# Two weight-sum additions per matrix made on GpSimd, in a two-layer decoder trunk with a seven-product feed-forward

## The chip, the cores and the metric

One core of a Trainium2 chip runs the whole program in one launch. The metric is device time in microseconds of that core, from the start of the program to its end. Five engines work side by side and meet through semaphores: TensorE (PE in the profile, with its weight loads as PEld), VectorE (DVE), ScalarE (ACT), GpSimd (POOL) and SyncE (SP). SyncE only issues transfers here; GpSimd issues transfers too, above all those that add what they bring to what lies in the tile already.

## The reference: what is computed

Two layers of a decoder trunk on 512 tokens of 1024 features, in float32. Each layer has a mixer stage (pooling, convolution and block-sparse attention behind one input projection) and then a feed-forward stage. Only the feed-forward is touched:

```python
h2 = rmsnorm(x, norm2_w) * (1 + sc2) + sh2
x = x + g2 * ((jax.nn.silu(h2 @ w_gate) * (h2 @ w_up)) @ w_down)
```

`w_gate` and `w_up` are 1024 x 2816, `w_down` is 2816 x 1024.

## The kernel before

Activations lie transposed, features on the 128 partitions and the 512 tokens along a row. Float32 products are made of three matmuls: every operand is split into a high part that TensorE takes exactly (`whi`, `hi`) and the rest (`wlo`, `lo`), and `mm3` (L157 issues the matmul) multiplies high by high, high by low and low by high. A weight tile holds eight blocks of 128 x 128. `split_w` makes the parts: ScalarE copies the tile to `whi` (L407), VectorE subtracts that from the tile to get `wlo` (L410). There are five `whi` and five `wlo` buffers, so ScalarE can split a tile only when TensorE has left the one five tiles back. Activations are split by `split_from` in the same way (L678 on ScalarE, L679 on VectorE).

**The feed-forward's parts.** The 22 column blocks of gate and up are worked off in four parts (`PARTS`). Most columns are taken two at a time by `glu_pair`: both matrices' 2 x 2 block products are made by seven half-size products in place of eight. Such a *pair* needs sums of weight blocks. The parts have one, three, two and three pairs, in each of the two layers: 18 pairs in all. Ten of them have another pair behind them, eight are the last of their part; behind those come the down products of the part.

**A pair on TensorE.** `glu_pair` runs 14 groups, for gate and up in turn: B21, B11, R1, -V, B22, T3, T4. A group is twelve matmuls on 256 columns. The products accumulate in PSUM banks `e`, `a` and `c`. Between them the banks are read and combined: L1430 and L1439 copy `a` on ScalarE, L1436 copies `c`, L1431, L1445 and L1449 add a bank to a tile on VectorE. L1449 reads the bank `a` after T3 and T4 then goes on accumulating in that same bank, first gate's, then up's. Then follow SiLU (L1457, L1458, L1459 on ScalarE) and the products with up (L1460, L1462, L1463 on VectorE), and the split of the result (L678, L679).

**The weight sums.** `Sums` makes four of the weight tiles of one matrix of a pair. `begin` lets GpSimd fetch one block row into half of `s12` and half of `s43` (L268) and add another to each on the way (L270). `first` fetches the raw blocks of the first tile on SyncE's queue and makes the two other halves with two additions on VectorE, 128 x 512 each: L276 adds raw blocks to the transferred sum, L277 adds the other raw blocks to that result. `first` is called once for gate and once for up, so a pair has four such additions and the program 72. `s12` is then split as the third and fourth weight tile of the pair (one for each matrix), `s43` as the fifth and sixth; the first two and the seventh are raw.

**What orders the work.** Each engine runs its instructions in the order in which a scheduler put them. Instructions wrapped in `pin` keep the order of the program among themselves, on their engine; the others are placed where the scheduler expects them to be ready. The additions were pinned on VectorE, as are the subtractions L410. A weight tile is loaded four tiles ahead of its use, and `begin` of a pair runs up to five tiles ahead of its first tile. The tiles `s12` and `s43` share six buffers (`w4`), the raw tiles three (`RAW`), so a transfer waits until the splits have left the buffer.

Of the kernel before, what the change touches and what calls it, by code (L numbers as in the profile page):

```python
# [85 lines left out]
def hybrid_trunk(ctx, tc, xT, ws, ada, cols, pool_w, qk_w, crow, pos, con, out):  # L86
    nc = tc.nc
    V, A, T = nc.vector, nc.scalar, nc.tensor
# [70 lines left out]
    def pin(ins):  # L159
        return tc.keep_in_program_order(ins)  # L160
# [83 lines left out]
    def fetch(tile, l, blocks):  # L244
        for i, n, src in runs(l, blocks):
            nc.sync.dma_start(tile[:, i:i + n].rearrange("p b n -> p (b n)"), src)
# [5 lines left out]
    class Sums:  # L252
# [19 lines left out]
        def first(self):  # L272
            raw = rawt()
            fetch(raw, self.l, self.blocks(0, 0) + self.blocks(1, 0))
            flat = raw.rearrange("p (g b) n -> p g (b n)", g=2)
            pin(V.tensor_add(self.s12[:, 1], self.s12[:, 0], flat[:, 0]))  # L276
            pin(V.tensor_add(self.s43[:, 0], self.s12[:, 1], flat[:, 1]))  # L277
            return split_w(raw, C_BLOCKS)

        def sums(self, which):  # L280
# [121 lines left out]
    def rawt():  # L402
        return wp.tile([P, C_BLOCKS, P], F32, tag="raw", name=nm("raw"), bufs=RAW)

    def split_w(raw, n):
        hi = wp.tile([P, C_BLOCKS, P], F32R, tag="whi", name=nm("whi"), bufs=5)
        A.activation(hi[:, :n], raw[:, :n], AF.Copy)  # L407
        lo = wp.tile([P, C_BLOCKS, P], F32R, tag="wlo", name=nm("wlo"), bufs=5)
        with tc.issue_after(hold[0].ins) if hold[0] is not None else nullcontext():
            ins = V.tensor_sub(lo[:, :n], raw[:, :n], f32(hi)[:, :n])  # L410
        pin(ins)
        return hi, lo
# [541 lines left out]
    for l in range(L):  # L954
# [438 lines left out]
        def make_forms(c):  # L1393

            h1, h2 = norm.h[c], norm.h[HK + c]
            one, two = bigt(F32), bigt(F32)
            t3, r1 = one[:, :BLOCK], one[:, BLOCK:]
            nv, t4 = two[:, :BLOCK], two[:, BLOCK:]
            V.tensor_sub(t3, h2[:, BLOCK:], h1[:, BLOCK:])
            V.tensor_sub(r1, h1[:, :BLOCK], h1[:, BLOCK:])  # L1400
            V.scalar_tensor_tensor(nv, t3, -1.0, h1[:, :BLOCK], op0=ALU.mult, op1=ALU.subtract)
            V.scalar_tensor_tensor(t4, nv, -1.0, h2[:, :BLOCK], op0=ALU.mult, op1=ALU.subtract)
            (a, al), (b, bl) = split_from(one), split_from(two)
            first, later = slice(0, BLOCK), slice(BLOCK, S)
            k1, k2 = norm.k(c), norm.k(HK + c)
            forms.append({"B11": cut(k1, slice(None), first), "B21": cut(k2, slice(None), first),
                          "B22": cut(k2, slice(None), later),
                          "T3": (a[:, first], al[:, first]), "R1": (a[:, later], al[:, later]),
                          "-V": (b[:, first], bl[:, first]), "T4": (b[:, later], bl[:, later])})
# [216 lines left out]
```

## Time and profile before

| | |
|---|---|
| median of two runs | 1433.36 us (1433.31 to 1433.4) |
| profiled execution, first to last instruction | 1431.7 us |
| median less that span | 1.7 us |
| granted TensorE clock in that execution | 1.000 |
| moved by the DMA engines | 245.51 MB, 171 GB/s on average |

A row of instructions in the profile reads: line, engine, operation, what it writes `<-` what it reads (the program's names), partitions x elements, how many; then busy time and the mean ns of one, and the idle time of the engine ahead of them with what ended it. A row of the timeline starts with the start time and the length in us; `x2` after it means two such instructions in a row, of which the length runs from the first start to the last end. Matmuls overlap each other, so a matmul's own length (0.28 us) is longer than the step from one start to the next, 0.12 us. A row of a window has the busy us of PE, PEld, DVE, ACT and POOL with the number of instructions, then the granted clock, the share of the DMA engines and GB/s.

### The profile page before, as it was taken

What the parts mean: (1) busy time and instruction counts of PE and PEld (TensorE: products, weight loads), DVE (VectorE), ACT (ScalarE), POOL (GpSimd) and SP (SyncE); (2) the same over time, 40 slices, a digit from 0 to 9 for tenths busy, and PEclk for the clock granted to TensorE, in tenths of its full rate; (3) what the DMA queues carried; (4) which work ended last, traced back from release to release, by engine and by line L of the source; (5) the groups of instructions that cost most, each with busy time, mean ns of one, the idle gap of its engine ahead of it and who ended that gap; (6) DMA issues with size and microseconds to landing.
All of it is one profiled execution on the core that took longest, in us unless ns stands there. A gap on an engine that the chain in (4) does not pass through costs nothing.

```text
span 1431.7 us, 22037 instructions
## 1 busy us (share of the span) xinstructions
PE 1426.4 (100%) x8340; PEld 1258.8 (88%) x8340; DVE 1038.3 (73%) x1904; ACT 731.3 (51%) x1229; POOL 153.2 (11%) x215
## 2 busy tenths in 40 slices
PE   9999999999999999999999999999999999999999
PEld 8888888888988998989988888888889989999997
DVE  8887777649686767677788996655878747657663
ACT  5635666733653452535454675666336525435450
POOL 0000110101100311211002000010020103111200
PEclk9999999999999999999999999999999999999999
DMA  9547876765346766756537665567672537636522
GB/s 372 207 147 210 217 189 164 191 220 164 91 141 217 192 175 206 186 144 207 187 103 234 174 152 143 133 163 179 257 206 85 141 103 193 175 105 176 139 89 83
DMA packets 92378, 245.51 MB, mean 171 GB/s; under 512 B 11752, under 2 KB 24432, under 8 KB 92272
## 3 DMA queue, kind: packets, MB, share of 16 engines
q1 hardware_dynamic: 67312, 177.37, 36.4%
q0 software_dynamic: 24368, 66.60, 23.3%
q8 instruction: 65, 1.06, 0.3%
q14 instruction: 41, 0.34, 0.1%
q10 hardware_dynamic: 592, 0.14, 0.0%
HBM read 241.97 MB, written 2.10 MB: 170 GB/s over the span
## 4 chain that ended last, share of the span: by engine, by line
PE 99%; DMA 0%; DVE 0%; SPq 0%; ACT 0%; issue 0%; DVEq 0%; ACTq 0%
PE mm L157 84%; PE pair L157 13%; PE mm L163 2%; DMA x<-in_xT 0%; SPq L203 0%; DVE w L513 0%; ACT big L665 0%; DVE big L917 0%; DVE big L907 0%; DVE tmp L661 0%; DVE x L1313 0%; ACT rst L932 0%; DVE rst L935 0%; DVE rst L934 0%; DVE rst L936 0%
## 5 line engine op out<-in xcount | busy, mean ns | idle before, releaser
L157 PE MATMUL mm<-big,whi 128*128 128x512 f32 (+1 forms) x4334 | 1072.9, 339 | 0.0
L157 PEld LDWEIGHTS mm<-big,whi 128*128 128x128 f32 x4334 | 741.4, 190 | 85.2 <-issue 2.6
L157 PE MATMUL mm<-big,wlo 128*128 128x512 f32 (+1 forms) x2167 | 732.0, 338 | 0.0
L157 PEld LDWEIGHTS mm<-big,wlo 128*128 128x128 f32 x2167 | 411.1, 190 | 45.0 <-issue 0.4
L407 ACT ACTIVATE whi<-raw 128x1024 fp32r<-128x1024 f32 (+2 forms) x190 | 195.9, 1034 | 199.3 <-PE mm L157 112.2
L410 DVE TENSOR_TENSOR wlo<-raw,whi 128x1024 fp32r<-128x1024 f32 (+2 forms) x190 | 223.5, 1187 | 43.8 <-ACT whi L407 43.3
L407 ACT ACTIVATE whi<-w 128x1024 fp32r<-128x1024 f32 x78 | 82.5, 1058 | 150.9 <-PE mm L157 91.5
L1313 DVE SCALAR_TENSOR_TENSOR x<-mm,mod,x 128x512 f32<-128x512 f32 (+1 forms) x89 | 61.5, 693 | 76.4 <-PE mm L157 76.3
L410 DVE TENSOR_TENSOR wlo<-w,whi 128x1024 fp32r<-128x1024 f32 x78 | 94.0, 1221 | 30.4 <-ACT whi L407 29.7
L513 DVE SCALAR_TENSOR_TENSOR w<-w,csil 128x1024 f32<-128x1024 f32 x80 | 95.7, 1220 | 13.9 <-DMA w<-in_ada 13.7
L268 POOL DMA_DIRECT2D w<-in_ws x72 | 46.6, 660 | 475.7 <-DVE wlo L410 278.5
L431 POOL DMA_DIRECT2D wlo<-in_ws x47 | 40.1, 854 | 401.9 <-ACT wlo L429 262.3
L270 POOL DMA_DIRECT2D w<-in_ws x72 | 63.2, 890 | 150.6 <-DMA w<-in_ws 148.3
L157 PE MATMUL pair<-whi,big 128*128 128x512 f32 x240 | 79.2, 389 | 0.0
L157 PE MATMUL pair<-big,whi 128*128 128x256 f32 (+1 forms) x392 | 78.9, 298 | 0.0
L157 PEld LDWEIGHTS pair<-big,whi 128*128 128x128 f32 x392 | 63.4, 191 | 2.8
L427 ACT ACTIVATE whi<-raw 128x1024 fp32r<-128x1024 f32 x47 | 50.1, 1066 | 30.6 <-PE mm L157 18.1
L157 PE MATMUL pair<-big,wlo 128*128 128x256 f32 (+1 forms) x196 | 58.4, 298 | 0.0
L157 PEld LDWEIGHTS pair<-whi,big 128*128 128x128 f32 x240 | 45.1, 188 | 9.3
L1270 DVE SCALAR_TENSOR_TENSOR big<-big,mm 128x512 f32<-128x512 f32 x48 | 32.6, 684 | 25.4 <-PE mm L157 24.8
L429 ACT ACTIVATE wlo<-whi 128x1024 fp32r<-128x1024 f32 x47 | 49.6, 1057 | 0.5
L679 DVE TENSOR_TENSOR big<-tmp,big 128x512 fp32r<-128x512 f32 x48 | 33.0, 691 | 21.3 <-ACT big L678 20.4
(244 smaller groups left out, 1402.6 us busy)
## 6 DMA issues: line engine op xcount, KB each, us to landing
raw<-in_ws SPq DMA_DIRECT2D x146, 512.0 KB, 4.3
w<-in_ada SPq DMA_DIRECT2D x80, 512.0 KB, 5.8
w<-in_ws POOLq DMA_DIRECT2D x144, 256.0 KB, 4.7
wlo<-in_ws POOLq DMA_DIRECT2D x47, 512.0 KB, 7.1
raw<-in_ws SPq DMA_DIRECT2D x64, 256.0 KB, 3.8
raw<-in_ws SPq DMA_DIRECT2D x24, 384.0 KB, 3.6
raw<-in_ada SPq DMA_DIRECT2D x16, 512.0 KB, 4.6
raw<-in_ws SPq DMA_DIRECT2D x16, 448.0 KB, 5.7
```

What stands on the lines that cost most here:

```text
L157: tc.keep_in_program_order(T.matmul(*a, **k))
L268: nc.gpsimd.dma_start(dst, self.source(0, 1))
L270: nc.gpsimd.dma_start(dst, self.source(*other), accum_op=ALU.add)
L407: A.activation(hi[:, :n], raw[:, :n], AF.Copy)
L410: ins = V.tensor_sub(lo[:, :n], raw[:, :n], f32(hi)[:, :n])
L427: A.activation(hi[:, :n], raw[:, :n], AF.Copy)
L429: A.activation(lo[:, :n], f32(hi)[:, :n], AF.Copy, scale=-1.0)
L431: nc.gpsimd.dma_start(lo[:, i:i + m].rearrange("p b n -> p (b n)"), src, accum_op=ALU.add)
L513: return V.scalar_tensor_tensor(aw, aw, 1.0, csil, op0=ALU.mult, op1=ALU.mult, accum_out=mod[l][:, part, j:j + 1])
L679: last_split[0] = V.tensor_sub(lo, src, f32(hi))
L1270: V.scalar_tensor_tensor(sg, sg, 1.0, branch, op0=ALU.add, op1=ALU.mult)
L1313: V.scalar_tensor_tensor(x[k][:, lo:hi], src, mod[l][:, part, k:k + 1], x[k][:, lo:hi], op0=ALU.mult, op1=ALU.add)
```

## The change

```diff
         def first(self):
             raw = rawt()
             fetch(raw, self.l, self.blocks(0, 0) + self.blocks(1, 0))
             flat = raw.rearrange("p (g b) n -> p g (b n)", g=2)
-            pin(V.tensor_add(self.s12[:, 1], self.s12[:, 0], flat[:, 0]))
-            pin(V.tensor_add(self.s43[:, 0], self.s12[:, 1], flat[:, 1]))
+            pin(nc.gpsimd.tensor_add(self.s12[:, 1], self.s12[:, 0], flat[:, 0]))
+            pin(nc.gpsimd.tensor_add(self.s43[:, 0], self.s12[:, 1], flat[:, 1]))
             return split_w(raw, C_BLOCKS)
```

The additions are the same; GpSimd makes them, in its own queue, among the transfers that it issues. TensorE and SyncE run the same instructions in the same order as before. On the other three engines the order around each pair changes. The following rows are of the first of three pairs in layer 1's second part (`tmp_12028` and `tmp_12044` are its gate and up), with the sums of the pair behind it (`w_11979` and `w_11980` are gate's first and second sum, `w_11985` and `w_11986` up's).

GpSimd, where that next pair's transfers end and those of the one after it begin:

```order
 L270 DMA w_11985<-in_ws 128x512
 L270 DMA w_11986<-in_ws 128x512
+L276 TENSOR_TENSOR w_11979<-w_11979,raw_12066 128x512
 L268 DMA w_12195<-in_ws 128x512
+L277 TENSOR_TENSOR w_11980<-w_11979,raw_12066 128x512
+L276 TENSOR_TENSOR w_11985<-w_11985,raw_12130 128x512
 L270 DMA w_12194<-in_ws 128x512
+L277 TENSOR_TENSOR w_11986<-w_11985,raw_12130 128x512
 L270 DMA w_12195<-in_ws 128x512
 L268 DMA w_12200<-in_ws 128x512
```

The four additions stand behind the last transfer that they need, and two transfers of the pair after next now stand between them.

ScalarE, at the end of the pair (`big_12238` is the high part of the first half of the result, `whi_12138` and `whi_12206` those of the next pair's first sums):

```order
 L1439 ACTIVATE tmp_12044<-mm_12043 128x256
 L1457 ACTIVATE tmp_12028<-tmp_12028 128x512
+L678 ACTIVATE big_12238<-tmp_12044 128x512
 L407 ACTIVATE whi_12138<-w_11979 128x1024
-L678 ACTIVATE big_12238<-tmp_12044 128x512
+L1458 ACTIVATE tmp_12075<-tmp_12075 128x256
 L407 ACTIVATE whi_12206<-w_11985 128x1024
-L1458 ACTIVATE tmp_12075<-tmp_12075 128x256
 L1459 ACTIVATE tmp_12075<-mm_12027 128x256
 L407 ACTIVATE whi_12250<-w_11980 128x1024
```

L678 and L1458 have each moved ahead of a split of the next pair's sums.

VectorE, at the same place:

```order
 L1460 TENSOR_TENSOR tmp_12044<-tmp_12044,tmp_12028 128x512
 L1449 TENSOR_TENSOR tmp_12075<-tmp_12075,mm_12027 128x256
+L679 TENSOR_TENSOR big_12239<-tmp_12044,big_12238 128x512
 L410 TENSOR_TENSOR wlo_12140<-w_11979,whi_12138 128x1024
 L1449 TENSOR_TENSOR tmp_12090<-tmp_12090,mm_12043 128x256
 L410 TENSOR_TENSOR wlo_12208<-w_11985,whi_12206 128x1024
-L679 TENSOR_TENSOR big_12239<-tmp_12044,big_12238 128x512
 L1462 SCALAR_TENSOR_TENSOR tmp_12090<-tmp_12090,tmp_12075 128x256
 L1463 SCALAR_TENSOR_TENSOR tmp_12090<-mm_12043,tmp_12075 128x256
```

L679 has moved ahead of two subtractions L410 and of the second L1449. The same happens, on both engines, in all ten pairs that have another pair behind them; in the eight last ones L678 and L679 stood there before, and their order does not change.

## The prediction

> **What bounds the kernel now.** I read the page's busy times and its chain first, then who waited for whom on TensorE, then one stretch of a pair on each engine.
>
> ```profile
> PE 1426.4 (100%) x8340; PEld 1258.8 (88%) x8340; DVE 1038.3 (73%) x1904; ACT 731.3 (51%) x1229; POOL 153.2 (11%) x215
> PE 99%; DMA 0%; DVE 0%; SPq 0%; ACT 0%; issue 0%; DVEq 0%; ACTq 0%
> ...
> PE pair L157 <- POOL ones L214: 1.1, 1, 1.1
> PE pair L157 <- ACT ccol L882: 0.3, 1, 0.3
> PE mm L157 <- ACT big L665: 0.2, 1, 0.2
> ```
>
> TensorE sets the end. The last three rows are the whole list of its waits: 1.6 us, all at the start. VectorE, which the change relieves, is on none of them. So the change can give next to nothing; the question is whether it makes TensorE wait.
>
> ```profile
> L277 DVE TENSOR_TENSOR w<-w,raw 128x512 f32<-128x512 f32 x36 | 24.8, 690 | 0.9
> L276 DVE TENSOR_TENSOR w<-w,raw 128x512 f32<-128x512 f32 x36 | 24.6, 684 | 0.0
> ...
> 1199.40:1219.60 20.20, 20.20 (x171) 20.20 (x170) 15.52 (x23) 11.53 (x18) 5.66 (x9) 1.00 0.74 184
> ```
>
> The first two rows are the edited lines: 72 additions, 49.4 us of VectorE. The third is one pair in the middle of a run of three (busy us of PE, PEld, DVE, ACT, POOL): TensorE needs all of its 20.2 us, VectorE 15.5.
>
> A pair is 14 groups of 12 matmuls on 256 columns; inside a group they start 0.12 us apart, so a group is 1.44 us. The last four are T3 of gate, T3 of up, T4 of gate, T4 of up. T4 of up accumulates in the bank that the second addition of L1449 reads, so it must wait for that addition. These are VectorE (first fence) and TensorE (second) in the first pair of a run of three, layer 1:
>
> ```profile
> 1190.40 1.23 DVE L410 TENSOR_TENSOR wlo<-raw,whi 128x1024 fp32r<-128x1024 f32 x1 [1.16 <-ACT whi L407]
> 1191.54 0.69 DVE L276 TENSOR_TENSOR w<-w,raw 128x512 f32<-128x512 f32 x1
> 1192.26 0.69 DVE L277 TENSOR_TENSOR w<-w,raw 128x512 f32<-128x512 f32 x1
> 1192.87 1.22 DVE L410 TENSOR_TENSOR wlo<-raw,whi 128x1024 fp32r<-128x1024 f32 x1
> 1194.01 0.74 DVE L1445 TENSOR_TENSOR tmp<-tmp,mm 128x256 f32<-128x256 f32 x2
> 1195.12 0.69 DVE L1460 TENSOR_TENSOR tmp<-tmp,tmp 128x512 f32<-128x512 f32 x1 [0.37 <-ACT tmp L1457]
> 1195.73 0.41 DVE L1449 TENSOR_TENSOR tmp<-tmp,mm 128x256 f32<-128x256 f32 x1
> 1196.21 1.22 DVE L410 TENSOR_TENSOR wlo<-w,whi 128x1024 fp32r<-128x1024 f32 x1
> 1197.35 0.41 DVE L1449 TENSOR_TENSOR tmp<-tmp,mm 128x256 f32<-128x256 f32 x1
> ```
>
> ```profile
> 1196.43 0.40 PE L157 MATMUL mm<-big,whi 128*128 128x256 f32 x2
> ...
> 1197.75 0.28 PE L157 MATMUL mm<-big,wlo 128*128 128x256 f32 x1
> 1197.87 0.46 PE L157 MATMUL mm<-big,whi 128*128 128x256 f32 x2
> 1198.16 0.28 PE L157 MATMUL mm<-big,wlo 128*128 128x256 f32 x1
> ```
>
> T4 of gate begins at 1196.43, T4 of up at 1197.87, 1.44 later. But the third matmul of T4 of up starts 0.29 after the first, where the rhythm gives 0.24: it slipped by 0.05 us. The second L1449 ended at 1197.76, so its word takes about 1197.92 - 1197.76 = 0.16 us to TensorE. **Here is the one place without slack:** whatever ends this L1449 later delays TensorE by as much.
>
> **The change, part by part.** *Removed from VectorE:* 72 additions, 49.4 us. On TensorE's path this is worth nothing except those slips, ten of 0.05, or 0.5 us at most; TensorE's own work covers the rest.
>
> *Added on GpSimd:* 72 additions, two inputs from SBUF. The trace has none of that kind, so I bound the price by GpSimd's nearest rows.
>
> ```profile
> L1102 POOL MEMSET tmp<- 128x256 f32 x2 | 0.6, 312 | 52.8 <-DVE ssq L720 50.0 <-DVE w L738 2.8
> L217 POOL TENSOR_SCALAR_AFFINE_SELECT mask<-mask 128x128 f32<-128x128 f32 x1 | 0.3, 292 | 0.0
> L216 POOL MEMSET mask<- 128x128 f32 x1 | 0.2, 199 | 0.0
> ```
>
> A write alone grows by 312 - 199 = 113 ns per 128 elements, so 512 would take 199 + 3 x 113 = 538 ns: the low end, 0.54. A read beside it adds 292 - 199 = 93 ns per 128. With two reads, 4 x (113 + 2 x 93) is 1196 ns, and the 86 fixed ns that are left of the memset (199 - 113) make it 1.28. The high end takes the whole select four times and doubles it, 2.34 us. I take 1.28; it is built of rows of the same engine.
>
> *Are the sums late?* The same pair, GpSimd, ScalarE and SP's two fetches of the raw blocks that these additions read:
>
> ```profile
> 1186.29 0.85 POOL L270 DMA_DIRECT2D w<-in_ws  x1 [0.36 <-DMA w<-in_ws]
> ...
> L268 POOL DMA_DIRECT2D w<-in_ws x72 | 46.6, 660 | 475.7 <-DVE wlo L410 278.5 <-DVE w L513 195.9 <-issue 0.6
> ...
> 1195.12 1.06 ACT L407 ACTIVATE whi<-w 128x1024 fp32r<-128x1024 f32 x1
> ...
> 1160.05 0.33 SPq L246 DMA_DIRECT2D raw<-in_ws  x1
> ...
> 1174.43 0.33 SPq L246 DMA_DIRECT2D raw<-in_ws  x1
> ```
>
> The raw blocks were fetched over 10 us earlier, so gate's additions run once the L270 of 1186.29 is off the engine, at about 1187.2. Moved order: addition, one L268, addition, addition, one L270, addition. At 1.28 each, with 0.66 and 0.85 for the transfers, gate's first sum is ready at 1188.5, up's at 1191.7, and the four end at 1193.8. Gate's first sum is needed by the split at 1195.12, up's a group (1.44 us) later, the second sums later still. Nothing is late, even at 2.34 (gate's first at 1189.5, up's at 1194.9). The transfers that now stand behind an addition (L268 and L270 of the next pair) land up to 6 us later, for a pair that starts 20 us later: hidden. Were that cover gone, each late sum would cost its own delay.
>
> *Moved on VectorE and ScalarE:* the scheduler also reorders the ten pairs that have another pair behind them. ScalarE does the activation copy L678 ahead of the split of the next pair's first sum; VectorE does L679, which needs L678, ahead of that split's subtraction L410, and only then the second L1449. The last pair of a run already has L679 in that place, and no additions ahead. Its rows show what the new chain takes:
>
> ```profile
> 1233.97 0.40 PE L157 MATMUL mm<-big,whi 128*128 128x256 f32 x2
> ...
> 1234.24 0.42 DVE L1445 TENSOR_TENSOR tmp<-tmp,mm 128x256 f32<-128x256 f32 x1 [1.02 <-PE mm L157]
> 1234.77 0.69 DVE L1460 TENSOR_TENSOR tmp<-tmp,tmp 128x512 f32<-128x512 f32 x1
> ...
> 1236.16 0.69 DVE L679 TENSOR_TENSOR big<-tmp,big 128x512 fp32r<-128x512 f32 x1
> ...
> 1235.50 0.63 ACT L678 ACTIVATE big<-tmp 128x512 fp32r<-128x512 f32 x1 [1.60 <-DVE tmp L1460]
> 1236.03 1.04 ACT L407 ACTIVATE whi<-raw 128x1024 fp32r<-128x1024 f32 x1
> ```
>
> Count from T3 of gate, here 1233.97. The second L1445 starts at +0.27, L1460 at +0.80, L678 at +1.53, the next split on ScalarE at +2.06. With the 1.06 of that split it ends at +3.12; its L410 starts 0.03 later, at +3.15; the next VectorE instruction starts 1.14 after an L410 does (1196.21 to 1197.35), so the second L1449 starts at +4.29 and ends, 0.41 later, at +4.70. Before, it ended at 1197.76, which from that pair's T3 of gate (1197.87 - 3 x 1.44 = 1193.55) is +4.21. **It ends 0.49 us later, and T4 of up with it.** The removed additions do not help: L1445 then starts when TensorE lets it, not earlier. Ten pairs: **+4.9 us**. The low bound is zero (L678 could slip in at no cost only if the split had waited for something else), the high bound comes with blocking, below.
>
> *Sum:* the profiled span 1431.7 + 4.9 = 1436.6. The median of the runs shown is 1433.36, 1.7 over the span, which stays: **1438.3 us**. A measurement tells about 2% from no change, 28.7 us, so I forecast no difference by that bound.
>
> **The rivals.**
>
> *The two engines block each other (6.3 us more).* In the six pairs that are first in a run the additions stand at 1187.2 to 1193.8 of the fences above, amid the L410 of 1190.40 and the next one. In the four middle pairs they come earlier against the tail:
>
> ```profile
> 1202.50 0.86 POOL L270 DMA_DIRECT2D w<-in_ws  x1 [0.47 <-DMA w<-in_ws]
> ```
>
> That is the last transfer ahead of them there; they end at about 1203.4 + 4 x 1.28 + 0.66 + 0.85 = 1210.0, and T3 of gate starts 20.2 us after 1193.55, at 1213.8. In a first pair, if no L410 can run while an addition reads, the L410 due at 1190.40 starts when up's first addition (1190.4 to 1191.7) ends; the next L410 follows 1.14 later, at 1192.8, and runs to 1194.1; then up's second addition takes 1194.1 to 1195.4. L1460, due at 1193.55 + 0.80 = 1194.35, can start at 1195.4. That is 1.05 us later, and all of it goes to T4 of up: 6 x 1.05 = 6.3, 1444.6 us. Against it: no row shows either engine slowed by the other, since GpSimd computes nothing in the pairs now. [...]
>
> *Nothing reaches TensorE.* The schedule's rows say order, not time; if ScalarE reaches the split early and the L1449 ends where it did, the time stays 1433.4 us. For it: 0.49 us is small. Against it: the slip of 0.05 shows that there is no slack.
>
> *Slower: VectorE runs out.* If every addition keeps VectorE out for its length, a pair costs VectorE 15.52 - 4 x 0.69 = 12.8 us plus four additions. It exceeds the 20.2 us of TensorE from 1.85 us an addition on. At the high end, 2.34, it is 12.8 + 9.4 - 20.2 = 2.0 us over, in ten pairs 20 us: 1438.3 + 20 = 1458.3. The 2% are passed at about 2.45 us. Against it: my 1.28, and VectorE is not always asking.
>
> *The relief pays.* TensorE gets back the slips and the new order costs nothing: 1433.4 - 0.5 = 1432.9 us.
>
> **How the numbers follow.** Forecast 0.43, blocking 0.27, nothing 0.17, VectorE runs out 0.10, relief 0.03. The forecast alone spans 1436 to 1441 (0.3 to 0.8 us in each of ten pairs). The range takes in blocking and "nothing" and part of the slow case: 1433 to 1448 us; outside lie the relief and most of the slow case, under 0.15. Slower by over 2%: 0.06, the upper part of the slow case. Faster by over 2% has no mechanism here, 0.01; the rest, 0.93, is within 2%.
>
> **What would show it.** Right: the additions on GpSimd at 1.0 to 1.6 us; VectorE's busy time about 49 us less; TensorE's list of waits with ten waits of T4 on L1449, some 0.5 us each, and no other new one. Blocking shows as L410 or L1460 rows of more than 1.3 or 0.8 us, or as idle time ahead of them without a releaser, while an addition runs. Wrong: no such waits (then the order was not the limit), or waits of TensorE for a split of a summed tile (then the sums come late, which I excluded), or additions beyond 2.4 us.

## The result, and the profile after

| | before | after |
|---|---|---|
| median of two runs | 1433.36 us | 1451.4 us (1451.3 to 1451.5) |
| profiled execution, first to last instruction | 1431.7 us | 1449.5 us |
| granted TensorE clock | 1.000 | 0.998 |
| predicted | | 1438.3 us (1433 to 1448) |

The change makes the kernel 1.25% slower: the ratio is 1.0125, interval 1.0106 to 1.0143. That is within 2%, as forecast, but 13 us above the forecast and 3 us above its range. The page of the changed kernel, and then TensorE's list of waits in it (us in total, times, longest), whose other rows are the three of before:

```profile
PE 1432.0 (99%) x8340; PEld 1260.8 (87%) x8340; DVE 1039.7 (72%) x1832; ACT 729.5 (50%) x1229; POOL 275.6 (19%) x287
```

```profile
PE mm L157 <- DVE tmp L1449: 8.6, 10, 1.2
PE mm L157 <- ACT tmp L1385: 3.8, 2, 1.9
```

The first row of waits is the place that the prediction named. The second is one that it did not name. And VectorE's busy time has not fallen, although 72 of its instructions are gone. The groups of additions and of subtractions L410 (128x1024) show why (first the L410 of before on a raw tile, then the changed kernel):

```profile
L410 DVE TENSOR_TENSOR wlo<-raw,whi 128x1024 fp32r<-128x1024 f32 x159 | 192.5, 1220 | 43.0 <-ACT whi L407 42.5
...
L410 DVE TENSOR_TENSOR wlo<-raw,whi 128x1024 fp32r<-128x1024 f32 x159 | 222.8, 1416 | 41.0 <-ACT whi L407 40.6
L410 DVE TENSOR_TENSOR wlo<-w,whi 128x1024 fp32r<-128x1024 f32 x78 | 97.8, 1269 | 34.5 <-ACT whi L407 34.5
L276 POOL TENSOR_TENSOR w<-w,raw 128x512 f32<-128x512 f32 x36 | 68.7, 1908 | 165.9 <-DMA raw<-in_ws 165.8
L277 POOL TENSOR_TENSOR w<-w,raw 128x512 f32<-128x512 f32 x36 | 62.4, 1733 | 1.7
```

The shortest GpSimd addition took 1.285 us, as priced, but the mean is 1.8 and the longest 2.36. The mean L410 on a raw tile has grown from 1220 to 1416 ns. Both engines are slowed, each by the other.

**Who holds whom.** At the end of part 0's columns in layer 0, VectorE (first fence) and GpSimd (second), one instruction a row:

```profile
402.66 1.22 DVE L410 TENSOR_TENSOR wlo<-raw,whi 128x1024 fp32r<-128x1024 f32 x1
403.80 1.52 DVE L1402 SCALAR_TENSOR_TENSOR big<-big,big 128x256 f32<-128x256 f32 x1
405.24 1.78 DVE L679 TENSOR_TENSOR big<-big,big 128x512 fp32r<-128x512 f32 x1
...
406.94 1.78 DVE L679 TENSOR_TENSOR big<-big,big 128x512 fp32r<-128x512 f32 x1
...
408.65 2.30 DVE L410 TENSOR_TENSOR wlo<-raw,whi 128x1024 fp32r<-128x1024 f32 x1
...
411.21 0.41 DVE L1400 TENSOR_TENSOR big<-big 128x256 f32<-128x256 f32 x1
```

```profile
403.23 1.80 POOL L276 TENSOR_TENSOR w<-w,raw 128x512 f32<-128x512 f32 x1 [35.60 <-DMA raw<-in_ws]
405.11 1.35 POOL L277 TENSOR_TENSOR w<-w,raw 128x512 f32<-128x512 f32 x1
406.43 1.74 POOL L276 TENSOR_TENSOR w<-w,raw 128x512 f32<-128x512 f32 x1
408.25 1.62 POOL L277 TENSOR_TENSOR w<-w,raw 128x512 f32<-128x512 f32 x1
```

Read the ends. The L410 ends at 403.88; the first addition, begun at 403.23, ends 1.15 us later, at 405.03. L1402, which alone takes 0.42, was begun at 403.80 and ends at 405.32, 0.29 after that addition. The second addition ends at 406.46, 1.14 after L1402. The first L679 ends 0.56 after it; the third addition 1.15 after that; the second L679 0.55 after it. In these rows the two engines take strict turns, each waiting out the whole instruction of the other.

**The tail of a pair.** In the first pair of the prediction's run of three (some 12 us later now), VectorE, GpSimd and TensorE:

```profile
1198.99 3.09 DVE L410 TENSOR_TENSOR wlo<-raw,whi 128x1024 fp32r<-128x1024 f32 x1
1202.70 3.85 DVE L410 TENSOR_TENSOR wlo<-raw,whi 128x1024 fp32r<-128x1024 f32 x2 [0.62 <-ACT whi L407]
1206.47 0.74 DVE L1445 TENSOR_TENSOR tmp<-tmp,mm 128x256 f32<-128x256 f32 x2
1207.58 0.69 DVE L1460 TENSOR_TENSOR tmp<-tmp,tmp 128x512 f32<-128x512 f32 x1 [0.36 <-ACT tmp L1457]
...
1208.96 0.69 DVE L679 TENSOR_TENSOR big<-tmp,big 128x512 fp32r<-128x512 f32 x1 [0.37 <-ACT big L678]
1209.91 1.23 DVE L410 TENSOR_TENSOR wlo<-w,whi 128x1024 fp32r<-128x1024 f32 x1 [0.26 <-ACT whi L407]
1211.06 0.41 DVE L1449 TENSOR_TENSOR tmp<-tmp,mm 128x256 f32<-128x256 f32 x1
```

```profile
1199.38 1.60 POOL L276 TENSOR_TENSOR w<-w,raw 128x512 f32<-128x512 f32 x1
...
1201.24 1.99 POOL L277 TENSOR_TENSOR w<-w,raw 128x512 f32<-128x512 f32 x1
1203.19 2.27 POOL L276 TENSOR_TENSOR w<-w,raw 128x512 f32<-128x512 f32 x1
...
1206.01 1.70 POOL L277 TENSOR_TENSOR w<-w,raw 128x512 f32<-128x512 f32 x1
```

```profile
1210.07 0.28 PE L157 MATMUL mm<-big,wlo 128*128 128x256 f32 x1
1211.53 0.51 PE L157 MATMUL mm<-big,whi 128*128 128x256 f32 x2 [1.18 <-DVE tmp L1449]
```

The L410 that alone take 1.22 take 3.09 and, two together, 3.85. L1445 stands behind them, L1457 behind L1445, L1460 behind L1457; then comes the moved order (L679 and an L410 ahead of the second L1449). TensorE waits 1.18 us and T4 of up comes 1.39 us late, where the order alone should make it 0.49.

**The second place.** End of part 0's columns: ScalarE before, then, in the changed kernel, ScalarE, TensorE, and windows over it (busy us of PE, PEld, DVE, ACT, POOL, then the granted clock):

```profile
407.98 1.17 ACT L1385 ACTIVATE tmp<-mm 128x512 f32<-128x512 f32 x2
409.17 0.63 ACT L678 ACTIVATE big<-big 128x512 fp32r<-128x512 f32 x1
```

```profile
406.67 1.06 ACT L407 ACTIVATE whi<-raw 128x1024 fp32r<-128x1024 f32 x1 [0.69 <-PE mm L157]
411.66 0.63 ACT L678 ACTIVATE big<-big 128x512 fp32r<-128x512 f32 x1 [3.93 <-DVE big L1400]
412.20 0.58 ACT L1385 ACTIVATE tmp<-mm 128x512 f32<-128x512 f32 x1
```

```profile
410.50 0.39 PE L157 MATMUL mm<-big,wlo 128*128 128x512 f32 x1
412.83 0.80 PE L157 MATMUL mm<-big,whi 128*128 128x512 f32 x2 [1.94 <-ACT tmp L1385]
```

```profile
412.50:414.50 2.00, 1.67 (x5) 1.36 (x6) 1.70 (x3) 2.00 (x4) 0.00 (x0) 0.71 0.56 212
414.50:416.50 2.00, 2.00 (x6) 1.52 (x6) 2.00 (x5) 0.86 (x2) 0.00 (x0) 0.50 0.10 22
416.50:418.50 2.00, 2.00 (x10) 1.64 (x9) 2.00 (x5) 1.71 (x4) 0.00 (x0) 0.93 0.76 226
```

L1385 (SiLU of a finished column) reads the PSUM bank that the next column's product is to use. In the new order, which the account of the change did not show for this place, an L678 of `make_forms` (it makes the sums of activations that the pairs need) stands ahead of it on ScalarE, and that L678 needs VectorE's L1400, which ran only at 411.21, behind the turns shown above. So ScalarE stands still for 3.93 us and TensorE for 1.94. Then a second loss follows: the granted clock falls to 0.50, and TensorE issues 6 matmuls in 2 us instead of 10.

**The sum.** TensorE issues the same 8340 matmuls in the same order in both kernels, so their starts can be set side by side; each step below is the growth of the difference over twelve matmuls, about a group. The six first pairs of a run lose 1.31 to 1.39 us each, 8.2 in all; the four middle pairs 0.47, 0.47, 0.46 and 1.01, 2.4 in all; the two ends of part 0's columns 3.8 each, 7.6 in all (2.1 and 2.0 in the step itself, 1.75 behind it at the low clock). With 0.3 us less at the start that is 17.9, and the two spans differ by 17.8.

### The profile page after: what moved, and what is told of

Read it like the earlier page. It is cut to its first block, busy times and chain, and to the rows that moved or that the text cites. A ratio compares the mean times of both kernels' runs of the same rounds, so it can differ in the third digit from the quotient of the medians.

```text
span 1449.5 us, 22106 instructions
## 1 busy us (share of the span) xinstructions
PE 1432.0 (99%) x8340; PEld 1260.8 (87%) x8340; DVE 1039.7 (72%) x1832; ACT 729.5 (50%) x1229; POOL 275.6 (19%) x287
## 4 chain that ended last, share of the span: by engine, by line
PE 91%; DVE 3%; ACT 2%; issue 2%; DMA 1%; POOL 1%; ACTq 0%; DVEq 0%; SPq 0%; POOLq 0%
PE mm L157 77%; PE pair L157 12%; PE mm L163 2%; ACT whi L407 1%; DVE wlo L410 1%; DMA raw<-in_ws 1%; DMA w<-in_ws 1%; ACT big L651 0%; DVE tmp L647 0%; DVE big L652 0%; POOL w L276 0%; DVE tmp L1449 0%; ACT big L655 0%; DVE tmp L1460 0%; POOL w L277 0%
## 5 line engine op out<-in xcount | busy, mean ns | idle before, releaser
L410 DVE TENSOR_TENSOR wlo<-raw,whi 128x1024 fp32r<-128x1024 f32 (+2 forms) x190 | 253.8, 1351 | 42.0 <-ACT whi L407 41.5
L410 DVE TENSOR_TENSOR wlo<-w,whi 128x1024 fp32r<-128x1024 f32 x78 | 97.8, 1269 | 34.5 <-ACT whi L407 34.5
L276 POOL TENSOR_TENSOR w<-w,raw 128x512 f32<-128x512 f32 x36 | 68.7, 1908 | 165.9 <-DMA raw<-in_ws 165.8
L277 POOL TENSOR_TENSOR w<-w,raw 128x512 f32<-128x512 f32 x36 | 62.4, 1733 | 1.7
L678 ACT ACTIVATE big<-tmp 128x512 fp32r<-128x512 f32 x48 | 29.9, 628 | 42.9 <-DVE tmp L1460 20.8
```

The costliest lines, as they stand in the source:

```text
L276: pin(nc.gpsimd.tensor_add(self.s12[:, 1], self.s12[:, 0], flat[:, 0]))
L277: pin(nc.gpsimd.tensor_add(self.s43[:, 0], self.s12[:, 1], flat[:, 1]))
L678: A.activation(hi, src, AF.Copy)
```

## The experiments

**The theory** was then: the moved order and the turns act together; at the tails order costs 0.47 and the turns the rest, at part 0 neither alone costs anything. **The rivals:** order alone, with the turns a bystander; the turns alone; and, for the low clock, GpSimd's work instead of the idle time. Lines of added code move the numbers of later lines by up to ten: L1453, L1451 and L1457 in waits of TensorE below are L1449, and L1387 and L1389 are L1385. The baselines that ran beside them had medians of 1433.3 to 1433.9 us.

**Order put back, one place at a time.** In the first of four kernels the additions stay on GpSimd and the tail has its old order, by edges to the splits of the next pair (`splits` collects the ScalarE and VectorE instructions of `split_w`):

```diff
...
-            A.activation(hi, src, AF.Copy)
-            last_split[0] = V.tensor_sub(lo, src, f32(hi))
+            with tc.issue_after(after[0].ins) if after else nullcontext():
+                A.activation(hi, src, AF.Copy)
+            with tc.issue_after(after[1].ins) if after else nullcontext():
+                last_split[0] = V.tensor_sub(lo, src, f32(hi))
...
-            A.activation(g2[:, BLOCK:], g2[:, BLOCK:], AF.Silu, scale=-1.0)
+            with nullcontext() if last else tc.issue_after(splits[-1][0].ins):
+                A.activation(g2[:, BLOCK:], g2[:, BLOCK:], AF.Silu, scale=-1.0)
...
-            act.append(split_from(u1))
+            act.append(split_from(u1, after=None if last else (splits[-2][0], splits[-1][1])))
```

> The additions stay on GpSimd, but at the end of the ten pairs with another pair behind them ScalarE and VectorE run L678, L1458 and L679 in the places that they had before the change. Theory (order and blocking together): the ten steps of T4 of up, 10.3 us in all, shrink to 0.0 to 0.1 us each, the idle of TensorE at the end of part 0's columns stays: 1451.4 - 9.8 = 1441.6 us. Rival 'blocking alone': only the 0.49 us of order go in each pair, the six blocked pairs keep 0.9 us each, 1451.4 - 4.9 = 1446.5 us. Rival 'order alone' says as the theory, about 1441.

Measured: 1443.2 us (ratio 1.0063, 1.0044 to 1.0082; single runs 1439.07, 1441.57, 1444.82 and 1445.12, the last one profiled). TensorE's waits in it:

```profile
PE mm L157 <- ACT tmp L1389: 5.0, 2, 2.9
...
PE mm L157 <- DVE tmp L1453: 1.0, 1, 1.0
```

Of the ten waits of T4 one is left; the two at part 0 have stayed, one of them longer than before (2.9 us). "The turns alone" falls for the tails: it wanted 0.9 us in each of six pairs. One pair in the profiled execution still loses 1.3 us, so the turns can reach TensorE there without the moved order too, but seldom. The median is 1.6 us above the expectation, and the runs are far apart: the mean granted clock is 0.996 in the slowest and 1.000 in the fastest, so in that one part 0 cannot have had the slow stretches. Why not is open, since only the slowest has a trace.

In the second kernel only part 0 has its old order:

```diff
...
-                    if k >= HK:
+                    if HK <= k < KT - 2:
                         make_forms(k - HK)
                 del held
+                early = [silu(f_ps[z]) for z in range(2)]
+                with tc.issue_after(early[1][1].ins):
+                    make_forms(HK - 2)
+                make_forms(HK - 1)
                 for z in range(FA):
-                    glu(f_ps[z], f_ps[FA + z])
+                    glu(f_ps[z], f_ps[FA + z], early[z][0] if z < 2 else None)
```

> The additions stay on GpSimd; only at the end of part 0's columns ScalarE runs the SiLU copies L1385 ahead of the splits L678 again, as before the change. Theory: L1385 reads a bank and waits for nothing of VectorE, so it is done in time; the idle of 1.9 us and the slow stretch behind it go in both layers, 7.5 us: 1443.9 us. Rival 'blocking alone': the late VectorE holds up something else of that place and TensorE idles there all the same, 1449 to 1451 us. Rival 'the clock dips for another reason than the idle (GpSimd's work, say)': only the idle itself goes, 3.8 us, 1447.6 us.

Measured: 1444.81 us (1.0077, 1.0062 to 1.0092). Its waits hold no L1385, and the ten at the tails are as in the changed kernel:

```profile
PE mm L157 <- DVE tmp L1453: 8.2, 10, 1.2
```

Windows over the end of part 0's columns, in layer 0:

```profile
409.00:411.00 2.00, 2.00 (x10) 1.68 (x9) 2.00 (x3) 0.58 (x1) 1.92 (x2) 1.00 0.22 46
...
413.00:415.00 2.00, 2.00 (x11) 1.65 (x10) 2.00 (x4) 0.63 (x1) 0.00 (x0) 1.00 0.00 0
```

Nothing is lost at part 0 in either layer any more, neither the idle nor the slow stretch behind it, while GpSimd's additions still run there (1.92 us of the first window). So these additions do not bring the clock down by themselves, and the idle is left as the cause; "The clock" below tests it alone.

Both edits together:

> Both places in the order of before, the additions on GpSimd. Theory: nothing is left but slips of at most 0.1 us in ten pairs, 1433.4 to 1434.4 us, with VectorE's rows beside the additions still stretched (L410 up to 3 us). Rival 'blocking alone': 1439 to 1446 us.

Measured: 1436.17 us (1.0015, 1.0006 to 1.0025; single runs from 1434.1 to 1437.2). The subtractions are as long as in the changed kernel,

```profile
L411 DVE TENSOR_TENSOR wlo<-raw,whi 128x1024 fp32r<-128x1024 f32 x159 | 222.7, 1415 | 44.2 <-ACT whi L408 43.6
```

yet 15.2 of the 18 us are gone. What remains is about 2.8 us, more than expected. The profiled execution, the slowest of the ten, has one tail with 1.3 us as above (another pair) and 1.2 us in layer 0's mixer (start of the attention part), where no addition runs. That place lost 0.8 us in the second kernel and nothing in the changed one; whether it belongs to the change is open. It does not beat the kernel before, and could not: TensorE has no more than its 1.6 us of waits to give.

**The turns taken away, the order kept.** GpSimd writes and reads nothing:

```diff
-            pin(nc.gpsimd.tensor_add(self.s12[:, 1], self.s12[:, 0], flat[:, 0]))
-            pin(nc.gpsimd.tensor_add(self.s43[:, 0], self.s12[:, 1], flat[:, 1]))
+            pin(nc.gpsimd.memset(self.s12[:, 1], 0.0))
+            pin(nc.gpsimd.memset(self.s43[:, 0], 0.0))
```

> GpSimd writes zeros to the two halves instead of adding, in the same places; the order on every engine is that of the changed kernel. This leaves out the two sums of each matrix. It separates order from blocking, because GpSimd reads nothing. Theory: VectorE's L410 go back to 1.22 us, VectorE's busy time falls to about 989 us, ten steps of 0.43 us are left and no idle at part 0: 1433.4 + 4.3 = 1437.7 us. Rival 'order alone': 1449 to 1451 us as in the changed kernel. Rival 'a GpSimd instruction of any kind holds VectorE up': L410 stretched by the write's length, 1442 to 1448 us.

Measured: 1439.09 us (1.0038, 1.0024 to 1.0052). But a write does not wait for the raw blocks, so at part 0 it ran earlier than the additions, and that place was not tested. The mended kernel has a one-column copy of the raw tile ahead of each write:

```diff
+            nc.gpsimd.tensor_copy(self.s12[:, 1, :1], flat[:, 0, :1])
+            pin(nc.gpsimd.memset(self.s12[:, 1], 0.0))
+            nc.gpsimd.tensor_copy(self.s43[:, 0, :1], flat[:, 1, :1])
+            pin(nc.gpsimd.memset(self.s43[:, 0], 0.0))
```

> As the kernel that writes zeros, but each write now waits for the raw blocks as the additions do (a one-column copy of the raw tile stands ahead of it), so that GpSimd works at the same times as in the changed kernel, at the end of part 0's columns too; the order on ScalarE and VectorE is that of the changed kernel. It leaves out the two sums of each matrix. Theory 'at part 0 too the order hurts only with VectorE shut out': no idle of TensorE for L1385, ten steps of 0.47 us at the tails, 1433.4 + 4.7 + 0.5 = 1438.6 us. Rival 'at part 0 the order alone does it': 1.9 us of idle and 1.75 behind it in each layer as well, 1446 us.

Measured: 1438.05 us (1.0035, 1.0021 to 1.0049). TensorE's waits, the subtractions, and ScalarE at part 0 in the new order:

```profile
PE mm L157 <- DVE tmp L1451: 2.7, 10, 0.3
```

```profile
L412 DVE TENSOR_TENSOR wlo<-raw,whi 128x1024 fp32r<-128x1024 f32 x159 | 192.3, 1220 | 61.6 <-ACT whi L409 61.1
```

```profile
408.48 0.61 ACT L680 ACTIVATE big<-big 128x512 fp32r<-128x512 f32 x1
408.99 0.58 ACT L1387 ACTIVATE tmp<-mm 128x512 f32<-128x512 f32 x1
```

The order on ScalarE and VectorE is that of the changed kernel. Ten steps of 0.46 to 0.48 us, 4.7 in all, and nothing at part 0: there the split still stands ahead of the SiLU copy, but finds its input at once. "Order alone" falls: it is 4.7 us of the 18. The writes, at the times of the additions, leave L410 at 1220 ns.

**One read in place of two:**

```diff
-            pin(nc.gpsimd.tensor_add(self.s12[:, 1], self.s12[:, 0], flat[:, 0]))
-            pin(nc.gpsimd.tensor_add(self.s43[:, 0], self.s12[:, 1], flat[:, 1]))
+            pin(nc.gpsimd.tensor_copy(self.s12[:, 1], self.s12[:, 0]))
+            pin(nc.gpsimd.tensor_copy(self.s43[:, 0], self.s12[:, 1]))
```

> GpSimd copies one half into the other (one input read) in place of each addition (two inputs read); everything else and the order as in the changed kernel. This leaves out the two sums of each matrix. Theory 'any read of GpSimd shuts out VectorE's instructions with two SBUF inputs': L410 is stretched as beside the additions, by up to the copy's own length (some 0.9 us by the same building blocks as the 1.28 of the addition), VectorE's busy time stands between the 998 us of the kernel that only writes and the 1040 us of the changed one, the time between 1439 and 1451 us. Rival 'only two reads at once do it': L410 at 1.22 us, 1439 us.

Measured: 1439.84 us (1.0047, 1.0030 to 1.0063), VectorE busy 1007.0 us. The copy's own row beside L410's:

```profile
L410 DVE TENSOR_TENSOR wlo<-raw,whi 128x1024 fp32r<-128x1024 f32 x159 | 197.4, 1253 | 54.9 <-ACT whi L407 54.6
...
L276 POOL COPY w<-w 128x512 f32<-128x512 f32 x36 | 37.2, 1033 | 2.1 <-DMA w<-in_ws 2.0
```

The 1253 ns of L410, where the writes left 1220, and VectorE's 1007.0 us, where they left 997.4, show that one read beside it costs VectorE time too. The time hardly differs from that of the writes: nine of the ten steps are 0.47 to 0.49 us, and one of the six first pairs loses 1.0. That the shorter copies mostly fit between VectorE's work is likely, but not shown; at part 0 they ran earlier than the additions, because they do not wait for the raw blocks. For the time this run does not decide between one read and two; for the rows it does.

**The clock.** Four kernels made from the kernel before, without GpSimd's additions: ScalarE keeps the awaited bank longer, by extra copies ahead of the SiLU copy, in part 0's order as above.

```diff
+        def silu(g, extra=0):
+            t = tmp()
+            for _ in range(extra):
+                A.activation(t, g, AF.Copy)
+            return t, A.activation(t, g, AF.Silu)
...
```

> The kernel before with nothing on GpSimd: at the end of part 0's columns ScalarE first copies the bank that TensorE waits for, four times in layer 0 and five times in layer 1, so that it comes free later; the places of the forms' splits L678 are behind it. A measured wait in place of the one that blocking made. Theory 'the idle alone brings the clock down, from somewhere between 1.3 and 2.0 us on': idles of about 0.5 and 1.1 us, nothing lost behind them, 1433.4 + 1.6 = 1435 us. Rival 'it needs the work of GpSimd as well': the same here.

> The same with six copies in layer 0 and seven in layer 1. Theory 'the idle alone brings the clock down': idles of about 2 to 3 us, behind each another 1.7 to 3.0 us lost in the next 7 us, granted clock near 0.6 there; 1433.4 + 5 + 4.5 = 1443 us. Rival 'it needs the work of GpSimd as well': only the idles, 1438.5 us, granted clock 1.0.

Measured: 1433.5 and 1433.56 us, beside 1433.34. No wait arose: the second SiLU copy went ahead of the extra ones and TensorE got that bank. These two tell nothing. With the second copy behind the first (`tc.issue_after`):

> As the two gap kernels before, but with both SiLU copies of the columns behind the extra copies (before, the second one went ahead and its bank was taken instead, so TensorE never waited): six extra copies in layer 0, seven in layer 1, and a split L407 among them. Idles of TensorE of about 1.6 and 2.2 us. Theory 'the idle alone brings the clock down, from somewhere between 1.3 and 2.0 us on': behind the second idle, and perhaps the first, some 1.7 us more are lost in the next 7 us, granted clock near 0.6: 1433.5 + 3.8 + 1.7 to 3.4 = 1439.0 to 1440.7 us. Rival 'it needs the work of GpSimd as well': only the idles, 1437.3 us, granted clock 1.0.

> The same with eight and nine extra copies: idles of about 2.7 and 3.3 us. Theory 'the idle alone': another 2 to 3 us lost behind each, 1433.5 + 6.0 + 5.0 = 1444.5 us. Rival 'it needs the work of GpSimd as well': 1439.5 us.

Measured: 1441.72 and 1445.03 us, beside 1433.94. The first of them, TensorE's wait in layer 0, and windows of 1 us:

```profile
412.78 1.11 PE L157 MATMUL mm<-big,whi 128*128 128x512 f32 x2 [1.97 <-ACT tmp L1387]
```

```profile
413.00:414.00 1.00, 1.00 (x3) 0.82 (x3) 1.00 (x3) 1.00 (x3) 0.00 (x0) 0.50 0.73 199
...
415.00:416.00 1.00, 1.00 (x4) 0.81 (x3) 1.00 (x3) 0.00 (x0) 0.00 (x0) 0.50 0.00 0
...
417.00:418.00 1.00, 1.00 (x6) 0.84 (x5) 0.92 (x2) 0.83 (x2) 0.00 (x0) 1.00 0.00 0
```

GpSimd does nothing here, and after 1.97 us of idle the clock stands at 0.50 for over 3 us, as in the changed kernel. The four waits of the two kernels, 2.0, 2.6, 3.2 and 3.9 us, were followed by losses of 1.72, 1.75, 2.77 and 1.75 us in the next 7. "It needs GpSimd's work" falls. The wait of 3.2 us cost more because its low clock lasted longer; in this window of the second kernel it is low where it stands at 1.00 above:

```profile
417.00:419.00 2.00, 2.00 (x6) 1.56 (x5) 1.97 (x5) 1.17 (x2) 0.00 (x0) 0.50 0.00 0
```

The clock's records in the traces give the lengths. Eight waits at part 0 (two each in the changed kernel, in the one with the tail's old order and in these two) were followed by a low clock: six times for 3.41 us, twice, after the waits of 3.2 and 2.9 us, for 6.83 us, which is twice 3.41. In the changed kernel's trace the two stretches begin 713.39 us apart, 209 times 3.4133. So cut that trace into such lengths. In the two just ahead of the low clock of part 0 TensorE stood idle for 1.94 and 1.84 us in all. No other length within the work has more than 1.18 us of idle, one at the end of the program has 1.51, and the clock stayed full after each of these. In the kernel whose wait of 3.2 us brought the 6.83 us TensorE was still idle when the clock was already low: for 0.90 us of the 2 us from 413 on, at 0.50. 3.41 us at half clock are 1.7 us lost, which is the 1.72 to 1.77 of the single ones.

## Why the prediction was wrong, point by point

- **What bounds the kernel: right**, but "the one place without slack" was one too few. The SiLU copy L1385 at part 0 has some 2 us to spare (in the kernel before the first one ended at 408.6, and the bank was due at 411), enough for the new order alone, not for the new order with VectorE held up. The prediction costed the tails of ten pairs and said nothing of the other instructions that the change moves, and the account of the change ahead of it named the pairs alone; that term was missing, and it measured 7.6 us.
- **The addition at 1.28 us: right** for one undisturbed (1.285). Among VectorE's work it takes 1.8 on average.
- **No sum late: right.** No wait of TensorE or ScalarE for a sum has appeared.
- **The moved order, 0.49 us in ten pairs: right.** With reads out of the way the ten steps measure 0.47 each, and the whole kernel 1438.05 us beside the forecast's 1438.3.
- **The choice between forecast and blocking: here it failed.** The forecast gave 0.43 to "no turns" and 0.27 to turns, on the ground that no row showed either engine slowed. But no row could: GpSimd computed nothing in a pair before. Absence from such a trace was no evidence. The changed kernel was the first to show both: L410 at a mean of 1416 ns in place of 1220, additions at 1.8 us where one undisturbed took 1.285.
- **That rival's size** was right where it was worked out: 6.3 us more, from six first pairs at 1.05 each. The six pairs measure 8.2 less 6 x 0.47, 5.4 us; one middle pair adds 0.5. Its path was near, not exact: it had L1460 right behind an addition, while in the rows two stretched L410 hold both L1445, and L1457 and L1460 follow. What it lacked was the second place.
- **VectorE's busy time 49 us less: wrong.** The waiting for a turn counts as busy, so 1039.7 stands where 989 was due; with the writes that read next to nothing it is 997.4, some 41 less (neighbouring instructions overlap, an L410 and the addition behind it by 0.09 us in the prediction's row of 1190.40, so 72 rows of 0.69 are not worth 49 us of busy time).
- **VectorE running out, at 1.85 us an addition:** the mean is at that mark, yet no pair became bound by VectorE; an addition does not keep VectorE out for its own waiting time (of the 1.80 us of the one at 403.23, 0.65 passed while an L410 ran).

The sum: 4.7 us of order, 5.9 us of turns at the tails (almost all of it only with the moved order), and at part 0 7.6 us for which both are needed, half of it idle time and nearly half the clock. Shown by the runs: that order alone costs 4.7 and nothing at part 0, that old order removes all but about 2.8 us, and that idle alone brings the clock down. Argued from rows only: the turn-by-turn account of single instructions.

## What to carry to other kernels

Here work moved to GpSimd was not out of VectorE's way where it read SBUF while VectorE ran instructions with two SBUF inputs (mean L410 1416 ns beside 1220, mean addition 1.8 us beside 1.285 for one alone): price each such meeting at the rest of the other's instruction, and follow it to the next queue that waits. When an edit lets a scheduler reorder an in-order engine, go through every place that it reordered, with the lateness that the edit itself may bring, not only through the place that looks tight. And price an idle of TensorE of 2 us at up to 3.8 in a kernel like this one: at part 0 a step of 2.1 us was followed by 1.75 more at a granted clock of 0.50.

## What the runs showed of the hardware

- **Turns:** in the rows at part 0 VectorE's two-input instructions and GpSimd's additions ran strictly one after the other (ends 0.29, 1.14, 0.56, 1.15, 0.55 us apart above). The mean L410 on a raw tile took 1220 ns beside writes, 1253 beside copies, 1416 beside additions. An L1445, with one input in SBUF and one in PSUM, was not held: two took 0.74 us at 1206.47, inside the addition of 1206.01 to 1207.71.
- **The clock:** waits of up to 1.2 us at the tails left TensorE's rhythm as it was (0.03 to 0.05 us lost in the next 7, in the changed kernel); waits of 1.9 us and more each brought the granted clock to 0.50 in the profiled executions and, in the changed kernel and the two of "The clock", cost 1.7 to 2.8 us more, by whether the low clock lasted 3.41 or 6.83 us. In the changed kernel's trace lengths of 3.41 us with 1.94 and 1.84 us of idle were followed by it, those with 1.51 and 1.18 were not.
- **GpSimd's prices** on 128 x 512 float32: writing 0.53 us (0.82 a row in the first of the two kernels that write, begun 0.47 apart), one read 1.03 in the mean, two reads 1.285 at the shortest; VectorE's addition took 0.69.
